# Reordered attention, a shorter lead of weight splits, and modulation steps placed later in a two-layer fp32 diffusion backbone

## The chip, the cores and the metric

The kernel runs on one core of a Trainium2 chip, as one program in one launch. The metric is the device time of one execution in microseconds. The kernel before took 2880.28 us, the median of 3 runs (2877.55 to 2882.24).

## The reference

Two layers act on 512 latent tokens and 256 context tokens of width 1024, all in fp32. A layer is an FFN, a token mixer and a second FFN. Each is modulated by vectors from a conditioning vector, and each is closed by a scaled residual and a layer norm:

```python
for i in range(DEPTH):                                   # 2 layers
    m_lat = modulation(c, w_mod[i], b_mod[i])            # 9 vectors of 1024: silu(c) @ w_mod + b_mod
    m_ctx = modulation(c_ctx, w_mod[i], b_mod[i])
    x = layer_norm(ALPHA * x + 0.5 * m[2] * swiglu(x * (1 + m[1]) + m[0], w_in, w_out))
    h = x * (1 + m[4]) + m[3]
    y = gqa_mix(h_lat, h_ctx, ...) if i == 1 else gmlp_mix(h, ...)
    x = layer_norm(ALPHA * x + m[5] * y)
    x = layer_norm(ALPHA * x + 0.5 * m[8] * swiglu(x * (1 + m[7]) + m[6], w_in, w_out))
```

The FFN is 2816 wide (22 tiles of 128). The gMLP of layer 0 has 3072 channels each way. The attention of layer 1 has 8 query heads, 2 key heads, heads of 128 elements, RMS-normed queries and keys and rotary positions; only the latent tokens have queries. After the attention the context tokens are not needed any more. The result is the latent stream.

## The kernel before, in words

**Precision.** Every fp32 matmul is three matmuls. Each operand is split into a high part (a cast on ScalarE) and a low part (a subtraction on VectorE): high times high, high times low, low times high. A weight tile of 128 x 512 split in this way is a "unit". There are 8 unit buffers (`W_BUFS`), 6 buffers for raw weights (`RAW_BUFS`) and a generator that yields units in the order of their use (`units`, line 276). `pump(n)` draws up to n units ahead while buffers are free; `weights(n)` takes units for use, `release(n)` gives their buffers back. A unit's low part is emitted only at the next `flush`.

**FFNs with 768 tokens.** The first three FFNs use a Strassen-like scheme with seven products a tile: five combined operands (T1 to T4, B22) are made from the modulated activations, beside the plain B11 and B21. `opening` (line 905) runs 12 half products of tiles 0 to 5 that need only B11 and B21, and after each of them one step of the generator `combine` (line 615) makes a piece of the combined operands on VectorE and ScalarE. Then `tile_strassen` (line 913) runs tile after tile; the first six ("opened") have five products left, the others seven. In the first FFN of the program a part of the opening lies in `start`. Each product is 4 x 3 matmuls of 128 x 384. After each product `slot` (line 155) emits, in this order, the low parts that are due, some units, perhaps a modulation step, and the evacuation of PSUM; while `combine` lasts, a step of it in place of the modulation. In these stages instructions are pinned: each engine executes them in the order in which the program emits them.

**Output projections.** `out_proj` (line 737) runs the second matmul in two halves of 512 columns. One slot x of a half is one weight unit times 6 token blocks, 18 matmuls of 128 x 512. Beside it, slots carry pieces of the residual (from the second sublayer on, ten of them in the odd slots of half 0), six additions at the head of half 1, or modulation steps. Of half 1 the last 6 units are kept for `End.inner` (line 1813), which closes one token block after the other: products, gated addition, statistics, rstd (a power on POOL, line 175), normalisation on ScalarE, transposes on TensorE, modulation to the next sublayer's operands.

**Modulation.** The vectors other than the first are made on VectorE behind the rest. `MOD_PLAN` (line 61) lists for each of the six sublayers which (layer, vector) it makes. A vector is 16 steps (`mod_unit`, line 349): load a 128 x 512 tile of `w_mod` ("mraw", 3 buffers, queue of SyncE), multiply it with the conditioning column, add to an accumulator ("acc"). Vectors up to (1, 4) have two conditions, and so two multiplies a step; those from (1, 5) on have one and are called light (`self.light`). After 8 steps POOL adds over the partitions (`partition_all_reduce`, line 372) and adds the row to DRAM. Shift and scale vectors are then read back as columns and turned on TensorE; `READ_LATER` and `TURN_LATER` count the calls of `fill` to these. `fill` (line 488) does one step; `fill_tile` (line 500) does two if the vector is light. A tile of an FFN calls it once, from the second tile on.

**Attention.** `attention` (line 1302) projects keys and values, then the queries of key head 0 (`q_proj(0)`), and changes the PSUM layout: two double banks ("pp") for scores and four single banks ("ps"). It transposes the keys of both heads (`k_transposed`, line 1356), and runs `q_proj(1)` in two groups of 3 and 1 token blocks (`token_proj`, line 1050). Between the groups `first_scores` transposes two query blocks and starts three units of scores and softmax. Then the loop over 32 units begins. At its end the output of key head 1 is closed like the other sublayers (`close`, line 726), and its 8 units are released after that.

Of the kernel before, what the change touches and what calls it, by code (L numbers as in the profile page):

```python
# [43 lines left out]

READ_LATER, TURN_LATER = 4, 7

# [16 lines left out]
    [(0, 5), (0, 6), (0, 7), (0, 8), (1, 0), (1, 1)],  # L63
    [(1, 5), (1, 2), (1, 3)],
    [(1, 4), (1, 6), (1, 7)],
    [],
# [19 lines left out]
class Backbone:  # L86
# [68 lines left out]
    def slot(self, post, n=1, fills=0):  # L155

        self.flush()
        self.pump(n)
        if self.combining is not None:
            post()  # L160
            if next(self.combining, self) is self:
                self.combining = None
        else:
            if fills:
                self.fill_tile()
            post()
# [332 lines left out]

    def fill_tile(self):  # L500

        self.fill()
        if self.light:
            self.fill()
# [220 lines left out]

    def close(self, b, banks, acts, ws, factor, st, first=True):

        n = len(acts)
        for half in range(2):
            self.products(banks[half], b, acts, ws[half * n : half * n + n], first)  # L730
        return [lambda half=half: self.add_gated(b, half, banks[half], factor, st) for half in range(2)]
# [5 lines left out]
    def out_proj(self, acts, l, i, factor, end, prev, gate_at=2):  # L737
# [9 lines left out]
        for half, order in enumerate(orders):  # L747
            body = n - CLOSE * half
            for x in range(body):
# [21 lines left out]
                if adds:  # L771
                    if x:
                        b, z, tmp = adds.pop(0)
                        self.dve.tensor_tensor(z, z, tmp, ALU.add)
                        self.dve.bn_stats(st[b][:, 0], z)
                    self.fill(int(prev is None or self.light))
                elif residual and x > 2 and (half or x % 2):
                    residual.pop(0)()
                    self.fill(int(self.light))
                elif half or x < n - 1:  # L780
                    self.fill()
        assert not residual
# [122 lines left out]
    def opening(self, seq):  # L905

        self.pin(True)
        self.combining = self.combine()
        for n, (f, half) in enumerate(seq):
            self.slot(self.open_half(f, half), 1 + int(n < 3))  # L910
            self.release(1)
# [49 lines left out]
    def ffn(self, l, i, nblocks, end, prev):  # L961
        if not self.begun:
            self.opening(OPEN)
        self.pin(True)
        acts = Acts(self, FF, TOK, KEPT, READ_BACK, f"act{l}{i}_")
        for f in range(FF):
            opened = self.begun.pop(min(self.begun)) if self.begun else None
            self.tile_strassen(lambda: acts.place(f), opened, int(f > 0))
            if not f:
                self.filler_raw()  # L970
        self.out_proj(acts, l, i, 0.5, end, prev, 2 if prev else 12)
# [78 lines left out]
    def token_proj(self, blocks, evacuate, fills=1, between=None):  # L1050
# [12 lines left out]
        elif between is not None:  # L1063
            groups = [blocks[:3], blocks[3:]]
            self.hooks = [between]
        else:
# [235 lines left out]
    def attention(self, l, i, nblocks, end, prev):  # L1302
# [134 lines left out]
        def first_scores():  # L1437
            for b in range(2):
                q_transposed(0, b)
            for n in range(AHEAD):  # L1440
                state[n] = softmax(*scores(n))

# [6 lines left out]
        q_tok.append([q1[:, b] for b in range(NB_LAT)])  # L1449
        for x in range(N_KV):  # L1450
            k_transposed(x)
        for b in range(2):
            q_norm(0, b)
        q_proj(1, between=first_scores)
        for b in range(2, NB_LAT):
# [54 lines left out]
        def closing(b):  # L1510
# [3 lines left out]
            banks = [self.bank(), self.bank()]  # L1514
            return self.close(b, banks, outputs(1), wo, 1.0, st[b]), st[b]

        end.run(NB_LAT, closing)
        self.release(8)

# [404 lines left out]
```

## Time and profile before

| | |
|---|---|
| median of 3 runs | 2880.28 us |
| the profiled execution | 2878.41 us, span 2876.6 us |
| mean granted clock of TensorE | 0.990 |
| TensorE (PE) busy | 2790.9 us, 97% |
| VectorE (DVE) busy | 2098.9 us, 73% |
| ScalarE (ACT) busy | 1160.1 us, 40% |
| POOL busy | 533.2 us, 19% |
| memory traffic | 148 GB/s over the span |

PE's busy time is modelled and matmuls are pipelined, so its idle time, not its busy time, is what can be read. In the timeline a row has its start, its length, the engine, the operation with its tiles and count, and in brackets the idle time just before it with what ended that. In a row of stretches the granted clock (1.00 is full) stands after the engine's busy time and count. `SPq` and `POOL ... DMA_DIRECT2D` are issues of transfers. All operations of pinned stages have line 81, so they are told apart by their tiles: `comb` are the combined operands, `w` the units, `ps` and `pp` the PSUM banks, `kT` and `qT` transposed keys and queries, `mraw` and `acc` modulation, `z` the residual stream.

### The profile page before, as it was taken

How to read it: one execution, taken by the hardware profiler on the slowest of the kernel's cores; microseconds unless marked ns; L12 is line 12 of the kernel's file. 1: busy time of each engine (PE TensorE's matmuls, PEld its weight loads, DVE VectorE, ACT ScalarE, POOL GpSimd, SP SyncE). 2: the span in 40 equal slices, each digit the busy share in tenths (PEclk: the TensorE clock that was granted, in tenths of full speed). 3: DMA queues.
4: the chain of work that ended last, by engine and by line, in shares of the span. 5: the costliest groups of instructions: out<-in, count | busy, mean ns of one | idle time of the engine just before them, and what ended most of it. 6: DMA issues, size and time to landing. Idle time of an engine off the chain costs nothing.

```text
span 2876.6 us, 40697 instructions
## 1 busy us (share of the span) xinstructions
PE 2790.9 (97%) x14454; PEld 2513.6 (87%) x14454; DVE 2098.9 (73%) x3692; ACT 1160.1 (40%) x2232; POOL 533.2 (19%) x605
## 2 busy tenths in 40 slices
PE   7899999999999999989999988999999989999998
PEld 6899988788899988889999878999988768888887
DVE  7988877587687786698887658988775588733445
ACT  6333332532355532543334235333432556633322
POOL 1010133233311142201012220111131121100001
PEclk9999999999999999999999999999999999999999
DMA  7433375355555474354336534433483523454352
GB/s 238 136 117 120 109 246 164 123 191 193 182 179 172 137 263 131 122 150 139 118 114 210 170 108 134 136 120 123 155 269 110 143 73 52 141 148 130 118 163 89
DMA packets 392339, 426.85 MB, mean 148 GB/s; under 512 B 28296, under 2 KB 281288, under 8 KB 392136
## 3 DMA queue, kind: packets, MB, share of 16 engines
q1 hardware_dynamic: 358024, 316.26, 35.4%
q0 software_dynamic: 34112, 108.00, 11.9%
q8 instruction: 113, 1.85, 0.3%
q14 instruction: 90, 0.74, 0.1%
HBM read 362.95 MB, written 63.41 MB: 148 GB/s over the span
## 4 chain that ended last, share of the span: by engine, by line
PE 86%; DVE 6%; ACT 3%; issue 2%; DMA 2%; POOL 1%; SPq 0%; DVEq 0%; POOLq 0%; ACTq 0%
PE ps L81 85%; PE pp L81 1%; DVE w L81 1%; ACT q L590 1%; DVE comb L81 1%; DVE z L81 1%; ACT z L1841 1%; DMA raw<-in_w_mod_dram 1%; DMA raw<-in_ffn_w_in_dram 1%; POOL acc L372 0%; POOL rs L175 0%; DVE q L81 0%; DVE w L148 0%; ACT h L590 0%; DMA mraw<-in_w_mod_dram 0%
## 5 line engine op out<-in xcount | busy, mean ns | idle before, releaser
L81 PE MATMUL ps<-comb,w 128*128 128x384 f32 x5544 | 982.0, 337 | 25.8 <-DVE comb L81 11.8
L81 PEld LDWEIGHTS ps<-comb,w 128*128 128x128 f32 x5544 | 970.6, 190 | 32.8 <-DVE comb L81 15.0
L81 PE MATMUL ps<-w,acts 128*128 128x512 f32 x3768 | 860.8, 390 | 0.0
L81 PEld LDWEIGHTS ps<-w,acts 128*128 128x128 f32 x3768 | 706.9, 188 | 146.4
L81 ACT CAST w<-raw 128x512 fp32r<-128x512 f32 x631 | 387.9, 620 | 860.7 <-PE ps L81 754.0
L81 DVE TENSOR_TENSOR w<-raw,w 128x512 fp32r<-128x512 f32 x631 | 456.3, 731 | 293.4 <-ACT w L81 293.4
L81 PE MATMUL ps<-h,w 128*128 128x384 f32 (+2 forms) x2304 | 445.4, 353 | 3.5 <-DVE w L148 3.5
L81 PEld LDWEIGHTS ps<-h,w 128*128 128x128 f32 x2304 | 402.4, 188 | 41.3 <-DVE w L148 3.9
L81 PE MATMUL ps<-w,h 128*128 128x512 f32 x1200 | 278.5, 393 | 6.9 <-DVE kT L142 4.1
L81 DVE SCALAR_TENSOR_TENSOR acc<-mraw,cs,acc 128x512 f32<-128x512 f32 x378 | 275.2, 763 | 6.7 <-DMA mraw<-in_w_mod_dram 6.5
L81 PEld LDWEIGHTS ps<-w,h 128*128 128x128 f32 x1200 | 226.9, 190 | 56.0 <-DVE kT L142 4.3
L372 POOL PARTITION_ALL_REDUCE acc<-acc x56 | 197.6, 3531 | 344.1 <-DVE acc L81 317.6
L81 DVE TENSOR_TENSOR q<-q,ps 128x384 f32<-128x384 f32 (+1 forms) x282 | 156.9, 556 | 125.6 <-PE ps L81 104.4
L81 POOL DMA_DIRECT2D q<-act x226 | 127.1, 595 | 556.8 <-DVE acts L81 317.5
L81 POOL DMA_DIRECT2D act<-stage x84 | 49.4, 588 | 948.5 <-DVE stage L81 898.5
L81 ACT CAST w<-sums 128x512 fp32r<-128x512 f32 x198 | 122.9, 621 | 246.9 <-DVE sums L291 131.5
L81 DVE TENSOR_TENSOR acts<-q,acts 128x384 fp32r<-128x384 f32 (+1 forms) x262 | 141.2, 572 | 6.0 <-ACT acts L81 5.9
L81 ACT CAST acts<-q 128x384 fp32r<-128x384 f32 (+1 forms) x262 | 125.9, 519 | 48.0 <-DVE q L81 38.3
L81 DVE TENSOR_TENSOR w<-sums,w 128x512 fp32r<-128x512 f32 x198 | 135.6, 685 | 3.0 <-ACT w L81 3.0
L148 DVE TENSOR_TENSOR w<-raw,w 128x512 fp32r<-128x512 f32 x113 | 74.7, 687 | 29.0 <-ACT w L147 28.6
L175 POOL TENSOR_TENSOR rs<-ve,mhalf 128x1 f32<-128x1 f32 (+3 forms) x47 | 40.7, 866 | 277.1 <-DVE ve L172 146.1
L147 ACT CAST w<-raw 128x512 fp32r<-128x512 f32 x113 | 67.7, 624 | 55.5 <-PE ps L81 30.3
(197 smaller groups left out, 2157.7 us busy)
## 6 DMA issues: line engine op xcount, KB each, us to landing
raw<-in_ffn_w_in_dram SPq DMA_DIRECT2D x388, 256.0 KB
mraw<-in_w_mod_dram SPq DMA_DIRECT2D x256, 256.0 KB
raw<-in_ffn_w_out_dram SPq DMA_DIRECT2D x176, 256.0 KB
q<-act POOLq DMA_DIRECT2D x216, 192.0 KB, 4.0
act<-stage POOLq DMA_DIRECT2D x74, 384.0 KB, 2.7
raw<-in_gmlp_w_in_dram SPq DMA_DIRECT2D x96, 256.0 KB
zhat<-z POOLq DMA_DIRECT2D x26, 512.0 KB, 2.9
raw<-in_gmlp_w_out_dram SPq DMA_DIRECT2D x48, 256.0 KB
```

Of the source, the lines that this page charges most:

```text
L81: return self.tc.keep_in_program_order(f(*args, **kwargs))
L147: self.act.copy(hi, src)
L148: self.lows.append((key, lambda: self.dve.tensor_tensor(lo, src, hi.bitcast(F32), ALU.subtract)))
L175: self.last_rstd = self.nc.gpsimd.tensor_tensor(rs, ve, self.mhalf[:, 0:1].to_broadcast([P, n]), ALU.pow).ins
L372: nc.gpsimd.partition_all_reduce(accs[c], accs[c], P, bass_isa.ReduceOp.add)
L590: self.act.activation(h32[:, kk], ps[:, s], AF.Identity, bias=bi, scale=sc)
L1841: k.act.activation(k.z[b], k.z[b], AF.Identity, bias=nb, scale=rs)
```

## The change

There are five edits.

1. `slot`: while combined operands are made, units are pumped only until three are ready (`LEAD`); the openings ask for two in each slot. Before, they asked for two in the first three slots and for one after, with no limit but the buffers.
2. Modulation steps in an FFN's tiles begin at tile 6 (tile 4 in the first FFN) rather than tile 1. In the output projections light vectors take two steps in a slot. Reading and turning of the columns come earlier after the reduction (2 and 4 rather than 4 and 7 calls).
3. (1, 5) is made in layer 1's first FFN rather than in layer 0's second FFN. The words of the change speak of a vector given to the gMLP, but the gMLP's list is the same before and after.
4. Attention: the second key head is transposed later, `q_proj(1)` runs in groups of 2, 1 and 1 blocks, two units of scores start after the first group, and the third with the second head's keys after the second.
5. At the attention's end four units are released, and new ones pumped, after each half of the last block.

```diff
-READ_LATER, TURN_LATER = 4, 7
+READ_LATER, TURN_LATER = 2, 4
+LEAD = 3
...
-    [(1, 5), (1, 2), (1, 3)],
-    [(1, 4), (1, 6), (1, 7)],
+    [(1, 2), (1, 3)],
+    [(1, 4), (1, 5), (1, 6), (1, 7)],
...
         self.flush()
-        self.pump(n)
         if self.combining is not None:
+            self.pump(max(0, min(n, LEAD - len(self.wready))))
             post()
             if next(self.combining, self) is self:
                 self.combining = None
         else:
+            self.pump(n)
             if fills:
-                self.fill_tile()
+                self.fill_pair()
             post()
...
-    def fill_tile(self):
+    def fill_pair(self):
...
-    def close(self, b, banks, acts, ws, factor, st, first=True):
+    def close(self, b, banks, acts, ws, factor, st, after=None):
         n = len(acts)
         for half in range(2):
-            self.products(banks[half], b, acts, ws[half * n : half * n + n], first)
+            self.products(banks[half], b, acts, ws[half * n : half * n + n])
+            if after:
+                after()
...
                 elif half or x < n - 1:
-                    self.fill()
+                    self.fill_pair()
...
-        for n, (f, half) in enumerate(seq):
-            self.slot(self.open_half(f, half), 1 + int(n < 3))
+        for f, half in seq:
+            self.slot(self.open_half(f, half), 2)
...
-            self.tile_strassen(lambda: acts.place(f), opened, int(f > 0))
+            self.tile_strassen(lambda: acts.place(f), opened, int(f > (5 if prev else 3)))
...
-            groups = [blocks[:3], blocks[3:]]
-            self.hooks = [between]
+            groups = [blocks[:2], blocks[2:3], blocks[3:]]
+            self.hooks = list(between)
...
-            for n in range(AHEAD):
-                state[n] = softmax(*scores(n))
+            sc = [scores(n) for n in range(PAIRS)]
+            for n in range(PAIRS):
+                state[n] = softmax(*sc[n])
+
+        def next_scores():
+            sc = [scores(n) for n in range(PAIRS, AHEAD)]
+            k_transposed(1)
+            for x in sc:
+                state[x[0]] = softmax(*x)
...
-        for x in range(N_KV):
-            k_transposed(x)
+        k_transposed(0)
         for b in range(2):
             q_norm(0, b)
-        q_proj(1, between=first_scores)
+        q_proj(1, between=(first_scores, next_scores))
...
+            after = None
+            if b == NB_LAT - 1:
+                def after():
+                    self.release(4)
+                    self.pump()
+            return self.close(b, banks, outputs(1), wo, 1.0, st[b], after), st[b]
         end.run(NB_LAT, closing)
-        self.release(8)
```

More of the change, by code (lines that the diff above doesn't have):

```diff
@@ L1514, in closing @@
             banks = [self.bank(), self.bank()]
-            return self.close(b, banks, outputs(1), wo, 1.0, st[b]), st[b]
+            after = None
[4 more added lines that the diff above has]
+            return self.close(b, banks, outputs(1), wo, 1.0, st[b], after), st[b]
         end.run(NB_LAT, closing)
-        self.release(8)
     def setup(self):
```

## The prediction

> **What bounds the kernel now.** I read the page first, then the list of TensorE's waits, then the timeline and the stretches around each long wait.
>
> ```profile
> PE 2790.9 (97%) x14454; PEld 2513.6 (87%) x14454; DVE 2098.9 (73%) x3692; ACT 1160.1 (40%) x2232; POOL 533.2 (19%) x605
> ```
>
> TensorE is the bound: 2790.9 of 2876.6 us. The change neither adds nor removes a matmul, so it can win only TensorE's idle time, 85.7 us, and the slow clock that follows some of it. The list of waits says whose fault the idle time is (total, times, longest):
>
> ```profile
> PE ps L81 <- ACT z L1841: 12.0, 8, 8.3
> PE ps L81 <- DVE comb L81: 11.8, 10, 2.3
> PE ps L81 <- DVE q L81: 7.2, 6, 4.0
> ...
> PE ps L81 <- ACT acc L81: 2.6, 2, 1.3
> PE ps L81 <- ACT q L81: 2.2, 2, 1.1
> PE ps L81 <- ACT comb L81: 2.0, 1, 2.0
> ```
>
> The "comb", "acc" and "q" rows belong to the three FFN openings and the tiles after them, and the 8.3 us to the end of layer 0's second FFN. The rest of what this change touches lies in the attention. I take the places in turn.
>
> **Part 1: the end of layer 0's second FFN.** POOL, then TensorE there, then TensorE at the end of the first FFN for comparison:
>
> ```profile
> 1696.83 3.66 POOL L372 PARTITION_ALL_REDUCE acc<-acc  x1 [15.23 <-DVE acc L81]
> ...
> 1705.13 0.79 POOL L373 DMA_DIRECT2D mod<-acc  x1 [0.30 <-POOL acc L372]
> 1713.09 0.59 POOL L175 TENSOR_TENSOR rs<-ve,mhalf 128x1 f32<-128x1 f32 x1 [7.17 <-issue]
> ```
>
> ```profile
> 1715.20 1.97 PE L81 MATMUL ps<-ident,z 128*128 128x128 f32 x8 [8.28 <-ACT z L1841]
> 1716.82 5.36 PE L81 MATMUL ps<-w,acts 128*128 128x512 f32 x17
> ```
>
> ```profile
> 546.69 1.09 PE L81 MATMUL ps<-ident,z 128*128 128x128 f32 x8 [0.75 <-ACT z L1841]
> 547.54 4.35 PE L81 MATMUL ps<-w,acts 128*128 128x512 f32 x18
> ```
>
> The last modulation step falls into the last slot of the output projection; its two reductions hold POOL, and the first rstd of the closing starts 7.17 us after POOL's last issue. By the code before, the slots are 21 tiles, 12 of the first half of the projection (its other ten slots carry the residual) and 7 of the second, 40 in all; the steps are 16 of the light vector (1,5), two to a slot, and 32 of (1,2) and (1,3): 8 + 32 = 40 slots. After the change (1,5) is gone and tiles 0 to 5 have no step: 16 + 12 + 7 = 35 slots for 32 steps, so the last step comes three slots earlier. A slot is 18 matmuls, 4.35 us by the last row, so 13 us earlier. From the first reduction's start to the rstd is now 1713.09 - 1696.83 = 16.3 us, and the rstd is wanted just after 1705.9 (POOL's last issue ended then); 13 us earlier it could start at 1700. The wait falls to the 0.75 of the other closing: 7.5 us. The slow clock goes too: eight transposes 1.97 against 1.09, 0.9 us, and 17 matmuls 5.36 against 17 x 4.35 / 18 = 4.11, 1.2 us. **9.6 us**, from 8 to 10.
>
> Does the 7.17 us move along, or is it paid wherever the next rstd is? At the gMLP's end the two reductions are followed by this:
>
> ```profile
> 1182.73 0.60 POOL L175 TENSOR_TENSOR rs<-ve,mhalf 128x1 f32<-128x1 f32 x1 [10.93 <-DVE ve L172]
> ```
>
> After 10.93 us of idleness the rstd started on its input, not on "issue": the time had run out in the idleness. With 13 us more, part 1 has that much too. The Trainium skill (GPSIMD Engine Reference, 2.1 Instruction dispatch) says that the first call to a freshly loaded kernel pays about 6 us without a visible instruction. By a strict reading the rstd would pay it wherever it stands; this is a rival below, and the row above speaks against it.
>
> **Part 2: modulation steps out of tiles 1 to 5.** The chain of waits (start, length), then TensorE in the last FFN with 768 tokens, then the granted clock by stretch (after PE's busy time and count; here for the attention too):
>
> ```profile
> 1254.05 4.99 DMA mraw<-in_w_mod_dram
> ```
>
> ```profile
> 1790.85 272.25 PE L81 MATMUL ps<-comb,w 128*128 128x384 f32 x1560 [1.89 <-DVE q L81]
> ```
>
> ```profile
> 1261.00:1264.00 3.00, 3.00 (x11) 0.50 0.63 179
> 1264.00:1267.00 3.00, 3.00 (x15) 0.75 0.28 82
> 1791.00:1794.00 3.00, 3.00 (x10) 0.52 0.90 271
> 1794.00:1797.00 3.00, 3.00 (x17) 0.91 0.32 95
> 2322.00:2325.00 3.00, 1.96 (x5) 0.50 0.25 87
> 2325.00:2328.00 3.00, 3.00 (x11) 0.66 0.00 0
> 2349.00:2352.00 3.00, 2.81 (x8) 0.50 0.00 0
> 2352.00:2355.00 3.00, 3.00 (x10) 0.61 0.01 3
> ```
>
> The first step's multiply waits on VectorE for a weight tile whose load is issued only when the first tile is done; everything behind it on VectorE waits too, the PSUM evacuations first, and TensorE after them. With the first step at tile 6 the same load has five tiles (over 50 us) to land. Nearly all of "DVE q" goes: 4.0, 1.9 and the small ones, say 6.8 of the 7.2. The clock loss is the missing share of each stretch: 3 x (0.50 + 0.25) = 2.2 and 3 x (0.48 + 0.09) = 1.7. **10.7 us**, from 8 to 11. The cover for the moved steps is tiles 6 to 21 and the projection. The Trainium skill (TensorE: Matmul & The Clock Gate, Part 1) drops the clock after an idle window of about 3.4 us; by it the 1.89 us wait would cost no clock and the sum would be 1.7 us smaller. The 0.52 behind that wait says otherwise, and I keep the row.
>
> **Part 3: three units of lead while operands are made.** In the openings of the two later FFNs TensorE waits 11.8 + 2.6 + 2.2 less what the first FFN has of it:
>
> ```profile
> PE ps L81 <- DVE comb L81: 5.6, 4, 2.3
> ```
>
> So 11.0 us in two openings, and 5.6 + 2.0 = 7.6 us in the first. VectorE is the reason:
>
> ```profile
> 1209.00:1250.00 41.00, 39.28 (x71) 1.00 0.42 124
> ```
>
> ```profile
> L81 DVE TENSOR_TENSOR w<-raw,w 128x512 fp32r<-128x512 f32 x631 | 456.3, 731 | 293.4 <-ACT w L81 293.4
> ...
> L81 DVE SCALAR_TENSOR_TENSOR acc<-mraw,cs,acc 128x512 f32<-128x512 f32 x378 | 275.2, 763 | 6.7 <-DMA mraw<-in_w_mod_dram 6.5
> ```
>
> Before, each opening runs about six units ahead (two pumped in each of the first three slots, then one); after, three. A unit of an opened tile costs VectorE a subtraction and 0.8 of a sum, 1.8 x 0.73 = 1.3 us, so 3 x 1.3 = 4 us of splits leave the opening and stand behind the operands. They are not saved: once the operands are made, two units are pumped per slot again, in tiles that keep VectorE about full. But in tiles 1 to 5 it loses five steps of two multiplies, 10 x 0.76 = 7.6 us, which more than holds them. Bounds: nothing (the waits only move into tiles 0 to 2) to all 11.0. I take a little over half, **6 us**. In the first FFN the operands' last parts are made only after the evacuations of tile 0, whatever the lead, so I take one wait before tile 0 and no more: **1.5 us**, from 0 to 7.6.
>
> **Part 4: attention.** TensorE:
>
> ```profile
> 2316.53 0.77 PE L81 MATMUL ps<-ident,p 128*128 128x128 f32 x5 [0.76 <-ACT q_tok L1333]
> 2317.97 0.98 PE L81 MATMUL ps<-ident,p 128*128 128x128 f32 x7 [0.67 <-DVE p L1322]
> 2323.04 18.48 PE L81 MATMUL ps<-w,h 128*128 128x512 f32 x72 [4.09 <-DVE kT L142]
> ...
> 2349.18 2.29 PE L81 MATMUL pp<-kT,qT 128*128 128x512 f32 x6 [3.59 <-ACT p L1392]
> ```
>
> Four banks are left; twelve key transposes fill them all, and the projection waits for VectorE to empty one. With one key head the six transposes take two banks, and the projection's first group, now two blocks, has the other two: the 4.09 goes, with 3 x (0.50 + 0.34) = 2.5 us of clock, of which about 2 is matmul time. Then the third score waits for the first softmax to free its pair. After the change one block's projection lies between, a third of the 72 matmuls or 6 us, longer than the 3.59: that goes, with 3 x (0.50 + 0.39) = 2.7 us of clock. Together 12.3. Against it: VectorE.
>
> ```profile
> 2341.00:2364.00 23.00, 22.14 (x46) 0.85 0.32 103
> 2331.00:2341.00 10.00, 0.63 (x3) 1.00 0.01 2
> ```
>
> It is full when the loop starts, but idle for 9.4 us just before, waiting for the group of three blocks; groups of two, one and one give it the same work earlier. So about 9.4 us can be taken from it, plus a little. **10 us**, from 4 to 12.3.
>
> The closing's early release: TensorE's first projection of the last FFN stood here:
>
> ```profile
> 2506.29 4.34 PE L81 MATMUL ps<-h,w 128*128 128x256 f32 x34 [3.33 <-DVE w L148]
> ```
>
> The splits now come ahead of the last block's additions. Three or four subtractions of 0.73 that go first delay that block's normalisation by 2 to 3 us, and TensorE's transposes of it come right after these 48 matmuls. **1.5 us**, from -1 to 3.3.
>
> **Part 5: pairs in the projection of layer 1's first FFN.** (1,5) comes here, so 48 light steps follow the 16 of (1,4), which now fill tiles 6 to 21. Half 0 gives 12 pairs and 10 single steps, 34; the other 14 end in the twelfth of the second half's 16 slots, and the columns are read and turned in the fourteenth and fifteenth. That is five slots, over 20 us, ahead of the first rstd with one reduction at a time, so part 1's stall does not return. The transfers gain 12 tiles of a quarter MB in about 90 us. I cost it at nothing, with 3 us for a late read or turn.
>
> **The sum.** 9.6 + 10.7 + 6 + 1.5 + 10 + 1.5 = 39.3 us. The profiled execution took 2878.41 us (span 2876.6), which makes 2839.1. It stands 1.9 us below the median of 2880.28, so I say 2840.
>
> **The rivals.**
> - *Attention stays VectorE's.* The 22.14 of 23 us is for it, the 9.4 us of idleness against. The loop's waits then eat the 10 us: 2850. Chance 0.13.
> - *The openings only move their waits* into tiles 0 to 2, since no split is saved: 7.5 us less, 2847.5. The lost steps of part 2 speak against it. 0.14.
> - *POOL pays its 7 us at the first rstd after any reduction*, however long before. Part 1 then yields almost nothing: 2849.6. The gMLP's row is against it. 0.04. This is the strict reading of the Trainium skill's page named in part 1.
> - *Slower: the lead is too short.* VectorE is 39.28 of 41 us busy; if its backlog passes three units (3 x 12 matmuls, about 6 us), each product waits on its own cast and subtraction. There are 12 + 6 x 5 = 42 such units in each of three FFNs, 126; at 0.5 us each 63 us, so 2903. It decides from 39.3 / 126 = 0.31 us a unit. Against it: the backlog before, with more work in front, cost about 5.5 us an opening. 0.05.
> - The words of the change name the gMLP, but its list of vectors is the same on both sides; (1,5) moves to layer 1's first FFN. I have costed the diff.
>
> **How the numbers follow.** The forecast has 0.64. If all the bounds came out well (all openings 11.0 + 7.6, attention 12.3, closing 3.3), it would be near 2823; the two mild rivals with a poor opening or attention beside them reach 2857. That range leaves out the slow rival and half of the joint mild ones. A difference of 0.2%, 5.8 us, is about what measurement can tell here. The forecast and the three mild rivals are all faster, 0.95; I take 0.02 off for what I have not seen, and split the slow rival's end: faster 0.93, same 0.03, slower 0.04.
>
> **What would show it.** Right: in layer 0's second FFN the last reduction ends well before the closing and no wait there passes 1 us; no wait on "mraw" before tile 6; the "comb" total under 7 us; no wait on kT, none of 3 us on the softmax; the clock at 1.00 in those places. Wrong: "PE ps <- DVE w" rows in the openings and tiles 0 to 2; a POOL "issue" of 7 us ahead of an rstd; more waits of the attention loop on softmax than before.

## The result and the profile after

The changed kernel takes 2856.01 us (median; 2850.79 to 2857.13) against 2879.81 us before on the same chip: 23.8 us less. The recorded ratio of the runs is 0.9908, 95% interval 0.9895 to 0.992 (the two medians alone would make it 0.9917); in a second measurement it was 0.9910 (0.9896 to 0.9923), 2853.70 against 2880.20 us. The forecast was 2840: faster as said, inside the range, but with some 24 to 26 us of the 39.3. A ratio of 0.9908 is 26.5 us of 2880, and the experiments below are told in the same way, as what the ratio takes off 2880 us.

The changed kernel's page, its line of busy times (span 2849.0 us):

```profile
PE 2780.5 (98%) x14454; PEld 2503.8 (88%) x14454; DVE 2110.9 (74%) x3692; ACT 1162.4 (41%) x2232; POOL 534.8 (19%) x605
```

The matmuls are the same in number; busy time fell by 10.4 us in this execution, with fewer of them at the slow clock (mean granted clock 0.996 after, 0.990 before). In a second profiled execution of the same kernel (e11, below) it fell by 6.1 us, to 2784.8, at a clock of 0.993, so a part of the 10.4 is this execution's luck. Its list of TensorE's waits (total, times, longest):

```profile
PE ps L83 <- DVE comb L83: 8.5, 7, 2.3
PE ps L83 <- DVE q L83: 6.1, 5, 2.2
...
PE ps L83 <- ACT z L1848: 4.3, 1, 4.3
...
PE ps L83 <- ACT z L1858: 3.1, 5, 0.8
...
PE ps L83 <- DMA s<-mod: 1.9, 1, 1.9
```

Compare it with the list before. The 8.3 us on z has gone (none there over 0.8 now). "comb" fell by a quarter only (the forecast named under 7), "q" by a sixth, and two rows are new: 4.3 us on another z and 1.9 us on the columns' DMA. Each belongs to one place.

Layer 0's second FFN, its end. GpSimd's timeline, then TensorE's:

```profile
1673.76 3.66 POOL L375 PARTITION_ALL_REDUCE acc<-acc  x1 [3.93 <-DVE acc L83]
...
1682.05 0.80 POOL L376 DMA_DIRECT2D mod<-acc  x1 [0.30 <-POOL acc L375]
1693.78 0.60 POOL L178 TENSOR_TENSOR rs<-ve,mhalf 128x1 f32<-128x1 f32 x1 [10.93 <-DVE ve L175]
```

```profile
1695.90 1.09 PE L83 MATMUL ps<-ident,z 128*128 128x128 f32 x8 [0.75 <-ACT z L1858]
```

The reductions end 11 us before the rstd, which starts on its input and not on "issue", and TensorE's 8.28 us are 0.75.

The same FFN's opening and its tiles 0 and 1 on TensorE:

```profile
1228.05 8.83 PE L83 MATMUL ps<-comb,w 128*128 128x384 f32 x49 [0.18 <-ACT acc L83]
1237.58 2.18 PE L83 MATMUL ps<-comb,w 128*128 128x384 f32 x11 [0.70 <-DVE comb L83]
1240.07 0.41 PE L83 MATMUL ps<-comb,w 128*128 128x384 f32 x1 [0.30 <-DVE q L83]
1241.78 8.42 PE L83 MATMUL ps<-comb,w 128*128 128x384 f32 x47 [1.31 <-DVE comb L83]
1252.36 37.87 PE L83 MATMUL ps<-comb,w 128*128 128x384 f32 x216 [2.16 <-DVE q L83]
```

The opening's waits are 2.5 us in all (0.18 + 0.70 + 0.30 + 1.31), where they were 5.7 us. But tile 1, the last row, still waits 2.16 us for VectorE. It was 3.99 in the kernel before:

```profile
1260.41 31.77 PE L81 MATMUL ps<-comb,w 128*128 128x384 f32 x168 [3.99 <-DVE q L81]
```

The attention:

```profile
2308.38 0.73 PE L83 MATMUL pp<-kT,qT 128*128 128x512 f32 x2 [0.74 <-ACT qT L143]
2310.52 1.91 PE L83 MATMUL pp<-kT,qT 128*128 128x512 f32 x10 [1.41 <-DVE qT L144]
2331.41 1.36 PE L83 MATMUL pp<-kT,qT 128*128 128x512 f32 x6 [2.06 <-ACT p L1397]
2362.27 0.87 PE L83 MATMUL ps<-ident,p 128*128 128x128 f32 x6 [1.57 <-DVE pT L144]
```

No wait on kT is left, and none of 3.6 us on the softmax; 2.06 us on it is the longest. And the end of the attention:

```profile
2479.59 1.97 PE L83 MATMUL ps<-ident,z 128*128 128x128 f32 x8 [4.32 <-ACT z L1848]
```

The 3.33 us on a weight operand became 4.32 us on the last block's z, just ahead of its transposes, which run at half speed (1.97 us for eight, 1.04 before).

**Where it came from.** The transposes of the z blocks stand in the same order in every kernel here, so the time between two of them measures a stretch. Five stretches, in us; the start up to 67.07 us is left out, it took 63.4 to 68.3 us in the profiles of all kernels. A column of several kernels is a mean, over the kernels named: "with" is the changed one, its repetition and the experiments that leave that stretch as changed; "without" is the kernel before and the experiments that leave it as before. The forecast is the prediction's terms sorted by place: part 2's 10.7 as 6.2 here, 3.6 there and 0.9 of small waits left out.

| stretch | without | with | gain | forecast |
|---|---|---|---|---|
| first FFN (67.07 to 546.69 before) | 479.6, 480.5, 482.6, 482.6: 481.3 | 480.9, 480.4, 481.0, 480.7: 480.8 | 0.5 | 1.5 |
| layer 0's second FFN (1218.87 to 1728.05) | 509.2, 508.1: 508.6 | 490.1, 490.2, 490.2, 490.1, 492.0: 490.5 | 18.1 | 9.6 + 6.2 + 3 = 18.8 |
| layer 1's first FFN (1751.46 to 2252.18) | 500.7, 501.1: 500.9 | 497.9, 498.2, 497.8: 498.0 | 2.9 | 3.6 + 3 = 6.6 |
| attention (2279.90 to 2487.16) | 207.3, 207.0, 204.8: 206.3 | eleven, 194.6 to 199.5: 197.6 | 8.7 | 10 |
| attention's end to the span's end (from 2499.84) | 376.8, 380.1, 378.3, 378.3, 378.3: 378.3 | seven, 379.0 to 382.1: 380.9 | -2.6 | 1.5 |

The sum of the gains is 27.6 us, which is what the ratio gives within its interval. The shortfall of 11 us lies in the last row (4), layer 1's first FFN (4) and the other three (about 1 each). That layer 0's second FFN came out nearly as forecast is partly luck: one edit brought more there than its term and two brought less, as the experiments show.

### The profile page after: what moved, and what is told of

It is laid out like the page before. It is cut to its first block, busy times and chain, and to the rows that moved or that the text cites. A ratio compares the mean times of both kernels' runs of the same rounds, so it can differ in the third digit from the quotient of the medians.

```text
span 2849.0 us, 40704 instructions
## 1 busy us (share of the span) xinstructions
PE 2780.5 (98%) x14454; PEld 2503.8 (88%) x14454; DVE 2110.9 (74%) x3692; ACT 1162.4 (41%) x2232; POOL 534.8 (19%) x605
## 4 chain that ended last, share of the span: by engine, by line
PE 83%; DVE 7%; issue 3%; ACT 3%; DMA 2%; POOL 1%; SPq 0%; DVEq 0%; POOLq 0%; ACTq 0%
PE ps L83 82%; DVE w L83 1%; DVE comb L83 1%; PE pp L83 1%; ACT q L593 1%; DMA raw<-in_ffn_w_in_dram 1%; POOL acc L375 1%; ACT z L1858 1%; DVE z L83 1%; DMA raw<-in_w_mod_dram 1%; DVE w L150 0%; ACT h L593 0%; DVE q L83 0%; POOL rs L178 0%; DVE nm L1389 0%
## 5 line engine op out<-in xcount | busy, mean ns | idle before, releaser
L83 PEld LDWEIGHTS ps<-comb,w 128*128 128x128 f32 x5544 | 962.6, 188 | 26.2 <-DVE comb L83 10.6
L375 POOL PARTITION_ALL_REDUCE acc<-acc x56 | 199.5, 3566 | 387.0 <-DVE acc L83 366.6
L83 DVE TENSOR_TENSOR acts<-q,acts 128x384 fp32r<-128x384 f32 (+1 forms) x262 | 148.0, 598 | 8.2 <-ACT acts L83 8.1
```

Of the source, the lines that this page charges most:

```text
L83: return self.tc.keep_in_program_order(f(*args, **kwargs))
L375: nc.gpsimd.partition_all_reduce(accs[c], accs[c], P, bass_isa.ReduceOp.add)
```

## The experiments

Twelve runs. Unless said otherwise the edit is against the changed kernel. The times:

| run | us | before, same chip | ratio (95%) | off 2880 us |
|---|---|---|---|---|
| e1_release_late | 2852.64 | 2880.28 | 0.9905 (0.9891 to 0.9918) | 27.4 |
| e2_no_lead_limit | 2854.70 | 2880.28 | 0.9913 (0.9899 to 0.9926) | 25.1 |
| e3_mod_early | 2857.53 | 2880.28 | 0.9919 (0.9906 to 0.9933) | 23.3 |
| e4_attn_alone | 2872.36 | 2880.28 | 0.9974 (0.9964 to 0.9984) | 7.5 |
| e5_plan_alone | 2871.10 | 2882.96 | 0.9964 (0.9951 to 0.9976) | 10.4 |
| e6_both_undone | 2855.06 | 2882.96 | 0.9909 (0.9894 to 0.9924) | 26.2 |
| e7_lead_5 | 2857.59 | 2882.96 | 0.9918 (0.9904 to 0.9931) | 23.6 |
| e8_turn_later | 2851.50 | 2882.96 | 0.9895 (0.9881 to 0.9908) | 30.2 |
| e9_plan_and_pairs | 2866.44 | 2880.20 | 0.9953 (0.9939 to 0.9967) | 13.5 |
| e10_three_mended | 2845.53 | 2880.20 | 0.9883 (0.9870 to 0.9897) | 33.7 |
| e11_changed_again | 2853.70 | 2880.20 | 0.9910 (0.9896 to 0.9923) | 25.9 |
| e12_mended_both_undone | 2853.66 | 2881.30 | 0.9900 (0.9883 to 0.9916) | 28.8 |

**The early release (e1).**

```diff
-            after = None
-            if b == NB_LAT - 1:
...
-            return self.close(b, banks, outputs(1), wo, 1.0, st[b], after), st[b]
+            return self.close(b, banks, outputs(1), wo, 1.0, st[b]), st[b]
         end.run(NB_LAT, closing)
+        self.release(8)
```

> The changed kernel with one thing undone: at attention's end the weight buffers are given back after the closing, as before, not within it. Theory A: the early release is a loss, because the splits that it lets VectorE and ScalarE do in the last block's closing stand ahead of that block's additions and normalization, and TensorE waits 4.32 us for the result in place of the 3.33 us it waited for a weight operand. By A the 4.32 us wait on ScalarE's z goes, the wait of about 3.3 us on a weight operand comes back, and the time is 1 us lower to equal: 2855 to 2856. Rival B (the prediction's step): the early release brings 1.5 us by itself, and the wait on z has another cause; then the wait on z stays near 4 us, the wait on the operand comes back beside it, and the time is 2857.5 or more.

2852.64 us. TensorE's timeline at the attention's end, without the early release:

```profile
2476.87 5.82 PE L83 MATMUL ps<-h,w 128*128 128x256 f32 x34 [3.33 <-DVE w L150]
2482.52 0.71 PE L83 MATMUL ps<-ident,z 128*128 128x128 f32 x5
```

The 4.32 us on z is gone and the old 3.33 us on the operand is back, so one wait stands for the other: rival B falls. In the time, e1 is not to be told from the changed kernel. The stretch table has more runs: with the early release the rest of the program takes 380.9 us, without it 378.3. The two waits differ by 1.0 us of these 2.6. Most of the rest fits the slow clock behind them: added up from the granted clock in stretches of 2 us, idle time included, the loss there is 1.4 us in the mean of the five kernels without the early release (none or 1.7 each), and 2.7 us in the mean of the seven with it (1.7 or 3.4 each).

**The limit of three units and the late modulation steps (e2, e3, e6, e7).** The prediction's parts 2 and 3 were tried alone, together and at another size.

```diff
-LEAD = 3
+LEAD = 99
```

> The changed kernel without the limit of three units on the splits while operands are made (the limit set so high that it never binds); all else as changed. Theory A (the prediction's part 3): the limit is worth some 7 us: the waits for VectorE's combined operands in the two later openings come back, and the time is 2862 to 2864. Rival B: the limit moves the waits from the openings to the tile behind them, where the splits that were held back fill VectorE (waits of 2.1 us on q at the second tile); by B those 2.1 us waits go when the limit goes, the openings' waits come back, and the time is within 2 us of 2856.

```diff
-            self.tile_strassen(lambda: acts.place(f), opened, int(f > (5 if prev else 3)))
+            self.tile_strassen(lambda: acts.place(f), opened, int(f > 0))
```

> The changed kernel with the modulation steps begun at the second tile of each FFN again, not at the fifth or seventh; all else as changed. Theory A (the prediction's part 2): the steps at tiles 1 to 5 cost some 10 us in three FFNs, waits on raw modulation weights and on q come back at tile 1, and the time is 2864 to 2867. Rival B: with the limit on splits in place, tile 1 waits for VectorE with or without the steps (2.1 us is still there), so the late start gives 4 us or less: 2856 to 2860.

2854.70 and 2857.53 us: neither is distinguishable from the changed kernel. e6 has both edits, on the suspicion that each stands in for the other:

> The changed kernel with both parts undone that lie at the FFNs' first tiles: no limit on the splits, and modulation steps from the second tile on. Each alone, undone, left the time within 2 us of the changed kernel's. Theory A: the two do the same work (they free VectorE at tiles 0 and 1), so each stands in for the other, and with both undone the waits of before are back (about 1.1, 1.3, 1.3, 0.7 and 1.1 us in each later opening, 4 us and 1.9 us at tile 1): 6 to 9 us above the changed kernel, 2862 to 2865. Rival B: they are worth little together as well, since the places where they help give back what they gain: within 3 us of the changed kernel, 2859 or less.

2855.06 us, and so the times said that 18 us of forecast were worth nothing. One thing is not undone in e2, e6 and, below, e12: the openings still ask for two units in every slot, where the kernel before did so in the first three only. The traces say a little more. TensorE at tiles 0 and 1 of layer 0's second FFN, first without the limit, then with the steps early, then with both undone:

```profile
1248.99 41.18 PE L83 MATMUL ps<-comb,w 128*128 128x384 f32 x236 [1.10 <-DVE comb L83]
```

```profile
1247.32 9.98 PE L83 MATMUL ps<-comb,w 128*128 128x384 f32 x47 [1.30 <-DVE comb L83]
1260.13 10.86 PE L83 MATMUL ps<-comb,w 128*128 128x384 f32 x60 [2.82 <-DVE q L83]
1271.54 18.79 PE L83 MATMUL ps<-comb,w 128*128 128x384 f32 x107 [0.55 <-DVE q L83]
```

```profile
1248.91 8.43 PE L83 MATMUL ps<-comb,w 128*128 128x384 f32 x47 [1.09 <-DVE comb L83]
1259.32 29.39 PE L83 MATMUL ps<-comb,w 128*128 128x384 f32 x168 [1.97 <-DVE q L83]
```

Without the limit, and with late steps, tile 1 doesn't wait at all (tiles 0 and on are one row of 236 matmuls). Adding up such rows for the two later FFNs gives TensorE's waits, in us:

| | openings | tile 1 | sum |
|---|---|---|---|
| before | 11.3 | 3.99 + 1.89 | 17.2 |
| vector (1, 5) moved alone (e5, below) | 11.4 | 2.33 + 2.09 | 15.8 |
| both undone (e6) | 11.5 | 1.97 + 1.79 | 15.2 |
| no limit, late steps (e2) | 11.5 | 0 | 11.5 |
| limit, early steps (e3) | 5.0 | 3.37 + 4.12 | 12.5 |
| limit, late steps (changed) | 5.0 | 2.16 + 2.14 | 9.3 |

The limit takes 6.5 us out of the openings, just as forecast (the two units a slot change nothing in the sum: 11.5 us in e6, 11.3 before), and puts some 4 back at tile 1, with early steps and with late ones alike. The late steps take 3.2 to 3.8 off tile 1. Together 6 us of waits, about a third of the forecast, and the stretches of the two FFNs agree: 494.1 and 499.2 us with both undone, 490.5 and 498.0 as changed, 4.8 us. Two things hide it in the times of e6. Its attention took 194.6 us, 3 less than the mean, because its clock never fell there, where it lost 1.7 us or more in every other kernel. And in layer 1's first FFN the late steps bring a wait of their own: TensorE waits 1.9 to 2.4 us for the columns' DMA in the changed kernel, e1, e2, e7 and e11, which all have late steps and the turn after four, and not at all in e3 and e6, whose steps are early. e12 repeats the comparison without that wait. A longer lead:

```diff
-LEAD = 3
+LEAD = 5
```

> The changed kernel with the limit at five units in place of three. Theory A: the wait of 2.1 us at tile 1 of the later FFNs comes from the splits that were held back, and the waits in the openings come from splits that were not; between three units and no limit there is a size that has less of both: the wait at tile 1 falls under 1 us while the opening's waits rise by less than 1.5 us, 2854 to 2856. Rival B: the sum of waits from the opening to tile 1 is VectorE's work alone and is not moved by the size: 48.4 to 49.8 us from the first transposes to tile 1 as at three units and at no limit, the waits only change their place, time equal within 1.5 us.

2857.59 us; in layer 0's second FFN 1.97 + 0.39 + 0.52 us in the opening and 1.82 us at tile 1, 4.7 in all, against 2.49 + 2.16 = 4.65 at three units; in layer 1's first FFN 5.6 against 4.65. Rival B: the waits change their place.

**Attention alone (e4).** The kernel before with the attention's hunks, without the early release.

```diff
-            groups = [blocks[:3], blocks[3:]]
-            self.hooks = [between]
+            groups = [blocks[:2], blocks[2:3], blocks[3:]]
+            self.hooks = list(between)
...
-        for x in range(N_KV):
-            k_transposed(x)
+        k_transposed(0)
...
-        q_proj(1, between=first_scores)
+        q_proj(1, between=(first_scores, next_scores))
```

> The kernel before with the attention's reorder alone (second key/value half's transposes and third pair's scores put behind the third projection block, both pairs' scores ahead of their softmaxes). Theory A (the prediction's part 4, at the size that the traces show from landmark to landmark): 8 to 10 us of the gain, 2870 to 2872. Rival B: the traces' 7.7 us at the attention are partly the operands that the earlier parts left ready; alone the reorder gives 4 us or less, 2876 or more.

2872.36 us, 7.5 us off (4.6 to 10.4), and 9.4 us shorter in its stretch. The median lies just above theory A's 2870 to 2872, and the interval leaves out rival B's 4 us or less: the gain is the attention's own.

**The vector moved alone, and with the pairs (e5, e9).** Against the kernel before:

```diff
-    [(1, 5), (1, 2), (1, 3)],
-    [(1, 4), (1, 6), (1, 7)],
+    [(1, 2), (1, 3)],
+    [(1, 4), (1, 5), (1, 6), (1, 7)],
```

> The kernel before with one part of the change alone: vector (1, 5) is made in layer 1's first FFN and no longer in the gMLP. Theory A (the prediction's part 1): 9.6 us go at the end of layer 0's second FFN, 2870 to 2871; the wait of 8.28 us on ScalarE's z there is under 1 us. Rival B: the 7 us that GpSimd takes before its first small instruction after the reductions are paid at another reduction's end or first small instruction, or the reductions are late in layer 1's first FFN in their turn, and TensorE waits there: 2876 or more, with a wait of over 5 us on another z.

2871.10 us, 10.4 us off. (The list that loses the vector is that of layer 0's second FFN, not the gMLP's.) Layer 0's second FFN fell by 13.9 us (509.2 to 495.3), more than theory A's 9.6, but layer 1's first FFN rose by 4.0. GpSimd, then TensorE, at the end of that FFN in e5:

```profile
2216.16 0.82 POOL L373 DMA_DIRECT2D mod<-acc  x1 [0.30 <-POOL acc L372]
2223.91 0.59 POOL L175 TENSOR_TENSOR rs<-ve,mhalf 128x1 f32<-128x1 f32 x1 [6.94 <-issue]
```

```profile
2226.02 1.97 PE L81 MATMUL ps<-ident,z 128*128 128x128 f32 x8 [3.31 <-ACT z L1841]
```

The stall has moved with the vector: 6.94 us of "issue" ahead of the first rstd, in the next FFN, because the light steps one by one again reach into the last slots. So B's mechanism is there too, at 4 us instead of 7. In the changed kernel the pairs would prevent it; e9 adds them:

```diff
-READ_LATER, TURN_LATER = 4, 7
+READ_LATER, TURN_LATER = 2, 4
...
                 elif half or x < n - 1:
-                    self.fill()
+                    self.fill_tile()
```

> The kernel before with two parts of the change: vector (1, 5) is made in layer 1's first FFN, and the light vectors' steps go in pairs in the output projection, with the columns read after two and turned after four steps. Against the run with the vector moved alone, which won 12.6 us at layer 0's second FFN by the trace and gave 4.0 back between the transposes before layer 1's first closing and its end. Theory A: the pairs are what gives those 4 us back (the last reductions come several slots before the closing): 2866 to 2868, no wait over 1 us on a z in that closing. Rival B (the prediction's part 5, pairs worth nothing): the loss there is the vector's own load of VectorE and remains: 2871, with the waits of up to 3.3 us on z still there.

2866.44 us, 13.5 us off (9.5 to 17.6). TensorE at the same place:

```profile
2221.49 1.09 PE L81 MATMUL ps<-ident,z 128*128 128x128 f32 x8 [0.75 <-ACT z L1841]
```

Layer 1's first FFN takes 499.1 us instead of 504.7. Theory A: the pairs, with the earlier read and turn, carry 3 us by the ratios and 5.6 by the stretch. Of the 5.6, 1.7 is a fall of the clock at tile 1 of e5 that e9 did not have, so about 4 are theirs, and they were needed only because the vector was moved.

Where do the other 4 us of e5's 13.9 come from? VectorE at tile 1 of layer 0's second FFN, before and in e5:

```profile
1256.64 0.48 DVE L81 TENSOR_SCALAR acc<-mraw,cs 128x512 f32<-128x512 f32 x1
...
1259.14 0.75 DVE L81 SCALAR_TENSOR_TENSOR acc<-mraw,cs,acc 128x512 f32<-128x512 f32 x1 [2.02 <-DMA mraw<-in_w_mod_dram]
```

```profile
1258.69 0.88 DVE L81 TENSOR_SCALAR acc<-mraw,cs 128x512 f32<-128x512 f32 x2 [0.60 <-DMA act<-stage]
```

Before, the FFN began with the light vector, whose two steps in a slot each need a weight tile of their own, and the second was 2 us late. With (1, 5) gone the first step multiplies one tile twice. So part 1's edit took the 3.99 us wait to 2.33, and its clock, that the prediction had given to part 2.

**Later turn, and the mended kernel (e8, e10, e11, e12).**

```diff
-READ_LATER, TURN_LATER = 2, 4
+READ_LATER, TURN_LATER = 2, 7
```

> The changed kernel with the modulation columns turned seven steps after their vector, not four (read after two, as changed). Theory A: the wait of 1.9 us that TensorE has on the columns' DMA in layer 1's first FFN goes, and nothing takes its place: 1.5 to 2 us less, 2854. Rival B: the DMA is late because the raw modulation weights and the steps themselves crowd the queues there, and a later turn finds the next step's raw weights late or meets the end of the FFN: a wait of like size elsewhere, 2856 or more.

2851.50 us, and 495.5 us for layer 1's first FFN against 498.0; the row "DMA s<-mod" is gone from the waits. Theory A, at 2.5 us by the trace. The wait needs both edits, the earlier turn and the late steps: e3, e6 and e9 turn after four as well, with early steps, and have none. e10 has this and two more edits:

```diff
-            self.pump(max(0, min(n, LEAD - len(self.wready))))
+            self.lead = lead or self.lead
+            self.pump(max(0, min(n, self.lead - len(self.wready))))
...
-            if after:
+            if after and not half:
                 after()
...
-            self.slot(self.open_half(f, half), 2)
+            self.slot(self.open_half(f, half), 2, lead=99 if seq is SECOND_OPEN else LEAD)
...
                     self.release(4)
-                    self.pump()
+                    self.pump(3)
...
         end.run(NB_LAT, closing)
+        self.release(4)
```

> The changed kernel with three edits that the runs so far point to: the columns turned seven steps after their vector in place of four; at attention's end four weight buffers given back after the last block's first half only, with three splits put there, the rest after the closing; no limit on the splits in the first FFN's opening, three units in the later ones. By the waits in the traces: 3.4 us less in layer 1's first FFN, some 2.5 less on z at attention's end (the 4.1 us wait falls under 2), some 1.5 less in the first FFN. Theory A, the waits add up: 2848 to 2850. Rival B: the wait at attention's end only changes sides (a wait of 3 us on the weight operand comes back) and the first FFN gains nothing: 2851 to 2852, as with the later turn alone.

> The changed kernel itself once more, beside the two others on one chip, so that they have their measure: 2856 within 2 us by both theories.

2845.53 us beside 2853.70 for the changed kernel on the same chip, ratios 0.9883 and 0.9910: it beats both kernels, and its slowest run (2850.55) is faster than the fastest of the changed kernel (2852.79). TensorE at the attention's end in e10:

```profile
2468.20 4.57 PE L83 MATMUL ps<-h,w 128*128 128x256 f32 x36 [0.16 <-DVE w L150]
2474.43 1.45 PE L83 MATMUL ps<-h,w 128*128 128x256 f32 x10 [1.66 <-DVE w L150]
2475.72 0.49 PE L83 MATMUL ps<-ident,z 128*128 128x128 f32 x3
```

Three splits ahead of the additions leave one wait of 1.66 us, for the operand, and none on z; the stretch to the end takes 376.9 us (375.1 in e12), against 380.9 as changed. A wait did change sides, as B had it, but at half its size. The first FFN took 479.8 us, 1 less, no more than its spread. Last, parts 2 and 3 once more, undone in the mended kernel:

```diff
-LEAD = 3
+LEAD = 99
...
-            self.tile_strassen(lambda: acts.place(f), opened, int(f > (5 if prev else 3)))
+            self.tile_strassen(lambda: acts.place(f), opened, int(f > 0))
```

> The kernel with the three mended edits, and in it both parts undone that lie at the FFNs' first tiles: no limit on the splits anywhere, and modulation steps from the second tile on. In the traces the two together save 4.0 us of layer 0's second FFN and 1.3 us of layer 1's first FFN; in the times they showed nothing (2855.1 undone, 2853.7 and 2856.0 with them). Theory A: the traces are right and the clock's chance hid it: 4 to 6 us above the mended kernel's 2845.5, 2850 to 2852. Rival B: what they save in the FFNs is given back elsewhere (the attention stands 1.5 us shorter in the runs without the limit): within 2 us of 2845.5.

2853.66 us (2851.72 to 2854.68; the mended kernel 2843.92 to 2850.55, on another chip), 4.9 us more by the ratios and 8.1 by the medians, though the two ratios' intervals overlap. In layer 0's second FFN it is 494.2 against 490.1 us, in layer 1's first FFN 501.6 against 495.5, of which 1.7 is a fall of the clock at tile 1 that the mended kernel did not have. Theory A is the nearer: in the mended kernel the two parts are worth some 5 to 8 us. e6 showed less because the wait for the columns ate 2 us of it and its clock was lucky.

## Why the prediction was right, and where not

- *Part 1, the end of layer 0's second FFN:* right, by its own steps. GpSimd's last issue now ends 10.93 us ahead of the rstd (13 by the forecast), the 7 us have run out by then, and the wait fell to the 0.75 named. Together with part 5 it measured 13.5 us (9.5 to 17.6) against 9.6, because it also took the light vector's late weight tile, counted in part 2. The rival that GpSimd pays its 7 us wherever the next rstd is falls in the changed kernel: its rstd started on its input after 10.93 us, as that at the gMLP's end had. e5 shows what the rival had of truth: the 6.94 us are paid again where a closing's rstd follows the last reduction at once. And "the time had run out in the idleness" is too wide a reading; the last section has a row against it. The Trainium skill (GPSIMD Engine Reference, 2.1 Instruction dispatch) gives about 6 us for the first call of a freshly loaded kernel; the measured 6.94 and 7.17 us are of that size. That a kernel is loaded there no row shows.
- *Part 2, the late steps:* failed at "Nearly all of 'DVE q' goes ... say 6.8 of the 7.2". It is 6.1 still. The late load was one cause of several; part 1's edit removed it. The steps themselves are another, and with the limit the splits that it holds back come due at the same tile: with late steps tile 1 doesn't wait at all without the limit (e2), and 4.3 us in two FFNs with it. Worth 3.2 to 3.8 us of waits, not 6.8, and the late steps brought the wait for the columns, about 2 us.
- *Part 3, the limit:* the 6 us for the two later openings were met (6.3 us of rows), but "tiles 1 to 5 lose five steps ... which more than holds them" failed: the splits that were held back are pumped before tile 1, and its evacuations wait for them, 4.3 us (nothing in e2). That is the second rival's mechanism: the openings move their waits into tile 1, mostly. In the first FFN the 1.5 us did not come; a wait of 1.26 us at tile 1 is new there, and it is absent in e2, e6 and e10, which have no limit in that FFN.
- *Part 4, attention:* right in mechanism and nearly in size, 8.7 us in the stretch and 7.5 alone against 10. In e9, with the attention of before, the clock lost 1.7 us in this stretch, as in most kernels with the new order, and it took 204.8 us: about 7 of the 8.7 us are waits, not clock. VectorE did not become the bound; against the gain stand waits that are new, 1.41 us on qT where two scores now follow each other and 1.57 us on pT. The *early release* had the wrong sign, -2.6 for 1.5. The delay of "three or four subtractions" was the mis-sized term: VectorE did eight, where one stood there before, since both halves pump what they can; this is its timeline in the changed kernel, with the last block's first product (L715) and its addition (L726) among them:

```profile
2468.76 3.69 DVE L150 TENSOR_TENSOR w<-raw,w 128x512 fp32r<-128x512 f32 x6
2472.38 0.68 DVE L715 SCALAR_TENSOR_TENSOR q<-ps,gate 128x512 f32<-128x512 f32 x1
2473.20 0.69 DVE L150 TENSOR_TENSOR w<-raw,w 128x512 fp32r<-128x512 f32 x1
2474.44 0.69 DVE L150 TENSOR_TENSOR w<-raw,w 128x512 fp32r<-128x512 f32 x1 [0.55 <-ACT w L149]
2475.05 0.68 DVE L726 TENSOR_TENSOR z<-z,q 128x512 f32<-128x512 f32 x1
```

- *Part 5, the pairs:* the 0 was two terms that cancel in part: the pairs carry 3 to 4 us of part 1's gain (e9 against e5), and the late turn that was allowed 3 us took 2.5 (e8), together with part 2's late steps.
- *The slow rival*, a lead too short: nothing of it. No row in the openings of the two later FFNs waits for a weight operand.

The forecast's error is thus the same wait counted twice over (part 2 and part 1; part 2 and part 3), and one edit that went wrong. In layer 0's second FFN the total hides this: the moved vector brought 13.9 us there (e5) for a term of 9.6, parts 2 and 3 the other 4 for terms of 9.2.

## What to carry over

When several edits relieve one engine at neighbouring places, don't add up their waits: write down what that engine does next after each, since work that is held back comes due at the first place where it is let go. Move work that is to be late in front of nothing that another engine waits for: three splits ahead of a normalisation delayed nothing here, eight cost a wait of 4 us. And ask of a step whose stall you remove where its own last instruction comes to stand after the move.

## What was not expected of the hardware

**The clock.** The granted clock falls in portions of about 1.7 us: added up in stretches of 2 us, its falls take 1.7, 3.4, 5.1, 6.8 or 8.5 us each, up to the program's last waits. In all, idle time included, that is 30.1 us in the profile before, 13.5 in the changed kernel's and 19.7 in its repetition. Whether a given wait costs a portion looks like chance. The attention's first projections follow a wait of 1.6 us in each kernel named here. In the changed kernel, and in the kernel before with the attention alone:

```profile
2259.19 34.14 PE L83 MATMUL ps<-w,h 128*128 128x512 f32 x141 [1.61 <-ACT h L607]
```

```profile
2283.91 32.54 PE L81 MATMUL ps<-w,h 128*128 128x512 f32 x141 [1.60 <-ACT h L604]
```

The same 141 matmuls, 1.6 us longer. The stretches of the changed kernel (granted clock after PE's busy time and count) show why:

```profile
2260.00:2264.00 4.00, 4.00 (x11) 0.61 0.15 22
2264.00:2268.00 4.00, 4.00 (x18) 0.97 0.49 149
```

4 x (0.39 + 0.03) = 1.68 us lost. It is 34.11 and 34.16 us in e1 and e2, 32.53 in e3 and in the kernel before, and 32.52 in e11, which is the changed kernel itself. The Trainium skill (TensorE: Matmul & The Clock Gate, Part 1) has a free-running activity window of about 3.4 us and half the clock after an idle one; half of 3.4 is 1.7, an estimate from the page's figure that agrees with the 1.68 measured, and a free-running window would explain that the same wait trips it or doesn't. But by its words the window must be idle, and here waits of 1.61 us were enough, sometimes. The same program's time hangs on it: the kernel before ran from 2875.37 us (mean clock 0.994) to 2882.73 us (0.990) in nine runs on one chip. The prediction gave the full clock loss to each wait it removed.

A portion ahead of a wait for another engine costs nothing. TensorE at tiles 0 and 1 of layer 1's first FFN, in e10 and in e11, which are alike there:

```profile
1758.39 8.43 PE L83 MATMUL ps<-comb,w 128*128 128x384 f32 x47 [1.30 <-DVE comb L83]
1768.97 31.31 PE L83 MATMUL ps<-comb,w 128*128 128x384 f32 x178 [2.16 <-DVE q L83]
```

```profile
1758.72 10.02 PE L83 MATMUL ps<-comb,w 128*128 128x384 f32 x47 [1.30 <-DVE comb L83]
1769.31 30.93 PE L83 MATMUL ps<-comb,w 128*128 128x384 f32 x176 [0.56 <-DVE q L83]
```

The slow matmuls of e11 took 1.6 us longer, the wait behind them is 1.6 us shorter, and tile 1 starts 10.6 us after tile 0 in both. So an edit of 2 us can be judged in the trace sooner than by the time, but by the starts of rows rather than by a wait alone: the 2.82 us of e3 stand behind such slow matmuls (9.98 us), and its sum of waits is 1.6 us too small.

**GpSimd's 7 us.** An "issue" of 7 us ahead of an rstd was to be a sign of a wrong forecast. One stands in every kernel here, before and after, in the middle of the gMLP, where TensorE doesn't wait. In the changed kernel:

```profile
762.61 3.26 POOL L1133 DMA_DIRECT2D v_spill<-q  x5 [9.92 <-ACT q L83]
766.02 0.54 POOL L1133 DMA_DIRECT2D v_spill<-q  x1 [0.15 <-issue]
773.48 1.37 POOL L178 TENSOR_TENSOR rs<-ve,mhalf 128x6 f32<-128x6 f32 x1 [6.92 <-issue]
```

The last reduction ended at 750.59. The 9.92 us of idleness behind it were a wait of the issue of a transfer, and they paid nothing: the rstd still had its 6.92 us (9.90 and 7.14 in the kernel before). In the rows with 10.93 us the rstd itself was the next in line. So, as far as these rows show, the 7 us begin only when the rstd is GpSimd's next instruction.

What stays open: what decides whether a wait costs a portion, and how the 26 us divide to better than about 2 us, since single stretches scatter by one or two such portions. Layer 1's first FFN in e12 and e6 is an example (501.6 and 499.2 us): e12 lost one portion at tile 1 and e6 none.
